# The state products of the first scan of a hybrid layer, as three one-pass products of split operands

## Chip, cores and metric

The kernel runs on one core of a Trainium2 chip. The metric is the device time of one execution in microseconds (us). Of each kernel several executions are timed, and their median is given. A separate execution is recorded by the hardware profiler, and all durations of single instructions come from it.

## What is computed

The reference is one layer of a hybrid decoder: 1024 tokens with 16 learned tokens ahead, model width 1024, all in float32. A state-space group (16 heads of 64, state size 128, in two groups of 8 heads) and an attention group stand side by side, their outputs are mixed by one matrix, and a gated feed-forward layer with a short convolution follows. What matters here is the state-space part, which works in chunks of 128 tokens (the 16 learned tokens are a short chunk of their own, chunk 0):

```python
states = jnp.einsum('bclgn,bgjcl,bclgjp->bcgjpn', Bc, decay_states, Xdt)
chunk_decay = jnp.exp(Acs[..., -1])
def step(carry, inp):
    st, dec = inp
    return carry * dec[..., None, None] + st, carry
_, prev = lax.scan(step, init, (states..., chunk_decay...))
y_off = jnp.einsum('bclgn,bcgjpn,bgjcl->bclgjp', Cc, prev, jnp.exp(Acs))
y = (y_diag + y_off).reshape(Bsz, Lp, H, P)[:, pad:]
```

For each group and chunk there are so two products with the state: `states`, from B and the decayed, time-scaled X of the chunk, and `y_off`, from C and the state before the chunk.

## The kernel before, in words

Everything is kept with channels or tokens on the 128 partitions. A large product such as x times a weight block is done on TensorE in the type fp32r, which takes one pass: each operand is split into a rounded part ("hi", a copy on ScalarE) and the rest ("lo", a subtraction, mostly on GpSimd), and hi·hi, lo·hi and hi·lo are summed in PSUM. `project_steps` (L165) is that loop for the projections, in three column blocks of 400, 384 and 256 tokens; `load_w` (L151, L152) splits the weights.

The scan of group g runs over chunks c = 0 to 8 in `scan_steps`, with three parts:

- `chunk_weights(g, c)`: builds the decay matrix of the chunk. Eight copies `sgh` on ScalarE (L615) and one product `sgl` on GpSimd (L617) are the two parts of a moving operand, TensorE sums them into `sg` (L624), ScalarE takes the exponential `em` (L626). TensorE also makes `cb` (L628), VectorE masks it to `cbm` and multiplies it into `em` (L630, L631). `xdt` (L634, VectorE) and `yo` (L637, GpSimd) scale the chunk's X.
- `chunk_outputs(g, c)`: `yf` = C times the state `prev` (L652), scaled to `yt` and added into `yo` (L654, L656); `xw` = decayed X (L660); `st` = B times `xw` (L663); the new state `pv` = old state times the chunk's decay (L668, GpSimd) plus `st` (L671, VectorE).
- `chunk_store(g, c)`: the product `yt` of `em` and `xdt` with the transposed `yo` added in PSUM (L682, L685), gated to `zk` (L689), squared to `sqk` (L692) and summed over heads (L694, L697), and stored.

The products `yf` and `st` have operands in plain fp32. The trace records each as two matmuls of 128x512.

The order of calls is: weights of chunk c+1, then one or two steps of other work, outputs of c, then one or two steps, store of c. The other work (`fill`) in the first group's scan is the projection, convolution (L465, L468 on VectorE, activation L470) and transposition (`tt_X`, L476, L481) of the second group's X blocks, then its z blocks; in the second group's scan it is the projection of q, k and v. So projections keep TensorE busy between the pieces of a scan. In this part of the program no order is written out by hand: the framework plans the order on each engine from its own estimates, with earlier calls first among those that it takes for ready. Later, the attention has TensorE's order by hand, and the feed-forward part that of four engines.

Buffers: the pool `sp` gives a tag one slot unless `bufs` says otherwise. `sgh` and `sgl` (128 x 1024 each) have one slot, `em`, `xdt`, `yo`, `xk`, `zk` and `prev` two. PSUM has two slots of tag `sd` for `yf` and `st`. The tags `bt`, `bn` and `ct` (B, B by tokens, and C) have one slot, and the second group's are written into it.

Of the kernel before, what the change touches and what calls it, by code (L numbers as in the profile page):

```python
# [9 lines left out]
F32 = mybir.dt.float32  # L10
F32R = mybir.dt.float32r
BF16 = mybir.dt.bfloat16
AF = mybir.ActivationFunctionType
ALU = mybir.AluOpType
# [3 lines left out]
P = 128  # L18
# [35 lines left out]
def tile_layer(ctx: ExitStack, tc: tile.TileContext, x, meta, rows, parts,  # L54
               w_z, w_xbc, w_dt, w_q, w_k, w_v, w_out, w_up, w_down, out):
    nc = tc.nc
    mm = nc.tensor.matmul
# [16 lines left out]
    def psum_sd(name):  # L74
        return stage[0][1].tile([P, 512], F32, tag="sd", name=name, bufs=2)
# [377 lines left out]
    with tc.tile_pool(name="ssd", bufs=1, side="right") as sp:  # L453
# [149 lines left out]
        def chunk_weights(g, c):  # L603
# [34 lines left out]
                                    op=ALU.mult)  # L638
            return em, xdt, yo

        def chunk_outputs(g, c, em, xdt, yo, prev):
            bt, bn, ct = state[g]
            nr = NM if c == 0 else P
            c0 = 0 if c == 0 else NM + (c - 1) * P
            hs = slice(8 * g, 8 * g + 8)
            nm = f"{g}_{c}"
            y0 = M0 if c == 0 else 0
            zk = sp.tile([P, 4, P], F32, tag="zk", name=f"zk{nm}", bufs=2)
            nc.sync.dma_start(out=zk[:, :, y0:nr], in_=zd[g][:, :, c0 + y0:c0 + nr].rearrange("b p t -> p b t"))
            if c > 0:  # L650
                yf = psum_sd(f"yf{nm}")
                mm(yf[:nr], ct[:, c0:c0 + nr], prev, start=True, stop=True)  # L652
                yt = sp.tile([P, 8, 64], F32, tag="yt", name=f"yt{nm}")
                nc.vector.tensor_tensor(yt[:nr], yf[:nr].rearrange("p (h d) -> p h d", d=64),  # L654
                                        eac[:nr, c, hs].unsqueeze(2).to_broadcast([nr, 8, 64]), op=ALU.mult)
                nc.vector.tensor_tensor(yo[:nr], yo[:nr], yt[:nr], op=ALU.add)  # L656
            nprev = None
            if c < NT:
                xw = sp.tile([P, 8, 64], F32, tag="xw", name=f"xw{nm}")
                nc.vector.tensor_tensor(xw[:nr], xdt[:nr],  # L660
                                        dec[:nr, c, hs].unsqueeze(2).to_broadcast([nr, 8, 64]), op=ALU.mult)
                st = psum_sd(f"st{nm}")
                mm(st, bn[:nr, c, :], xw[:nr].rearrange("p h d -> p (h d)"), start=True, stop=True)  # L663
                nprev = sp.tile([P, 512], F32, tag="prev", name=f"pv{nm}", bufs=2)
                if c == 0:
                    nc.vector.tensor_copy(nprev, st)
                else:
                    nc.gpsimd.tensor_tensor(nprev.rearrange("p (h d) -> p h d", d=64),  # L668
                                            prev.rearrange("p (h d) -> p h d", d=64),
                                            cdec[:, c, hs].unsqueeze(2).to_broadcast([P, 8, 64]), op=ALU.mult)  # L670
                    nc.vector.tensor_tensor(nprev, st, nprev, op=ALU.add)  # L671
            return yo, zk, nprev
# [29 lines left out]
        def scan_steps(g):  # L702
            cur = chunk_weights(g, 0)
            prev = None
            yield
            for c in range(NT + 1):
                nxt = chunk_weights(g, c + 1) if c < NT else None
                yield
                yo, zk, prev = chunk_outputs(g, c, *cur, prev)
                yield  # L710
                chunk_store(g, c, cur[0], cur[1], yo, zk)
                cur = nxt
# [364 lines left out]
    def psum_fa(name):  # L1077
        return stage[0][1].tile([P, 2, 512], F32, tag="fa", name=name, bufs=3)
# [8 lines left out]
    op = opool.enter_context(tc.tile_pool(name="outp", bufs=2, side="right"))  # L1087
# [13 lines left out]
    acc = psum_fa("halo1")[:, 0, 0:256]  # L1101
# [688 lines left out]
    for s in range(n2):  # L1790
        n, a, b, p = steps2[s]
# [29 lines left out]
        for _ in range(2 if s > 5 and s % 2 else 1):  # L1821
            if wload and (wload[0][0] is not None or s > 5):
                pool, nm, k = wload.pop(0)
# [87 lines left out]
```

## Time and profile before

| What | us |
|---|---|
| median of three executions | 1728.21 |
| lowest, highest | 1726.89, 1728.25 |
| profiled execution | 1726.21 |
| its span, from the first to the last instruction | 1724.3 |
| granted TensorE clock, mean | 0.998 |

The profile counts an engine as busy when an instruction of it runs; register, semaphore and DMA-issuing instructions don't count. PE is TensorE's matmul side, PEld its weight loads, DVE is VectorE, ACT is ScalarE, POOL is GpSimd. A line such as "L652" is the line of the kernel. In a view of waits, "A <- B" says that A's engine stood idle until B ended. In a timeline a row is one instruction or a few alike: its start, its duration, its engine. Matmuls are pipelined, so that two rows may overlap; the distance from one start to the next tells what a matmul costs in a stream.

### The profile page before, as it was taken

To read this page: it belongs to the slowest core of one execution; us is meant where nothing else is said; L and a number is where in the kernel's file an instruction comes from. 1 tells how busy PE (TensorE), PEld (TensorE's weight loads), DVE (VectorE), ACT (ScalarE), POOL (GpSimd) and SP (SyncE) were. 2 spreads that over 40 slices of the span, in tenths; PEclk is the share of its full clock that TensorE was granted. 3 is DMA by queue.
4 is the path that set the end of the run, shared out by engine and by line. 5 is a ranking of instruction groups with operands and counts; after the bars stand their busy time and mean duration, and the time that the engine had idled before them with its cause. 6 is when DMAs were issued, how large, how long until landed. Compare 5 with 4: busy or idle time off the path is not lost. (4 is left out here: it accounts for less than half of the span.)

```text
span 1724.3 us, 28047 instructions
## 1 busy us (share of the span) xinstructions
PE 1703.0 (99%) x11230; PEld 1496.2 (87%) x11230; DVE 1117.8 (65%) x1233; ACT 821.2 (48%) x1370; POOL 850.4 (49%) x642
## 2 busy tenths in 40 slices
PE   7999999999999999999999999999999999999998
PEld 6999889888999998998788788999888888887886
DVE  5752973875676677578530567676666666658777
ACT  5423663555566566557652344433333333344544
POOL 4323664585566575565552122587767777400001
PEclk9999999999999999999999999999999999999999
DMA  4233343231011101112214653233332223395334
GB/s 164 58 111 98 105 127 108 68 105 38 26 38 38 36 28 38 38 50 86 64 68 147 212 174 123 73 107 110 103 92 92 92 92 99 118 330 180 105 113 179
DMA packets 90674, 173.87 MB, mean 101 GB/s; under 512 B 10704, under 2 KB 35816, under 8 KB 90544
## 3 DMA queue, kind: packets, MB, share of 16 engines
q1 hardware_dynamic: 90544, 172.08, 31.4%
q8 instruction: 88, 1.44, 0.4%
q14 instruction: 42, 0.34, 0.1%
HBM read 122.32 MB, written 49.73 MB: 100 GB/s over the span
## 5 line engine op out<-in xcount | busy, mean ns | idle before, releaser
L782 POOL TENSOR_TENSOR bt<-bt,kp 128x256 f32<-128x256 f32 (+7 forms) x128 | 213.0, 1683 | 185.7 <-DVE kp L780 144.3
L780 DVE TENSOR_TENSOR_SCAN kp<-kp,hold 128x272 f32<-128x272 f32 (+7 forms) x128 | 183.5, 1474 | 24.7 <-ACT kp L773 14.3
L1265 POOL TENSOR_TENSOR wlo<-wr,whi 128x1024 fp32r<-128x1024 f32 x43 | 107.7, 2516 | 37.8 <-ACT whi L1264 37.8
L1768 POOL TENSOR_TENSOR fms<-fms 128x1 f32<-128x1 f32 x8 | 2.6, 331 | 223.8 <-ACT dh L1653 197.1
L773 ACT ACTIVATE kp<-z 128x288 f32<-128x288 f32 (+6 forms) x112 | 82.6, 737 | 50.5 <-PE z L772 27.8
L1264 ACT ACTIVATE whi<-wr 128x1024 fp32r<-128x1024 f32 x43 | 45.6, 1060 | 111.5 <-PE fX L1322 67.9
L165 PE MATMUL pj_k<-xs,wh_k 128*128 128x400 f32 (+2 forms) x384 | 95.6, 336 | 0.0
L165 PE MATMUL pj_v<-xs,wh_v 128*128 128x400 f32 (+2 forms) x384 | 95.0, 334 | 0.0
L1394 DVE SCALAR_TENSOR_TENSOR ga<-gr,pp,ga 128x1024 f32<-128x1024 f32 x44 | 71.8, 1632 | 35.1 <-ACT ga L1387 34.3
L165 PE MATMUL pj_q<-xs,wh_q 128*128 128x386 f32 (+2 forms) x384 | 93.8, 331 | 0.0
L796 ACT ACTIVATE th<-tw 128x1024 f32<-128x1024 f32 (+2 forms) x96 | 75.6, 815 | 37.4 <-PE tw L794 37.3
L1653 ACT ACTIVATE dh<-ar 128x512 fp32r<-128x512 f32 x77 | 48.6, 631 | 92.9 <-PE dnB L1731 44.7
L165 PE MATMUL pj_X<-xs,wh_X 128*128 128x400 f32 (+2 forms) x384 | 92.0, 326 | 0.0
L165 PE MATMUL pj_z<-xs,wh_z 128*128 128x386 f32 (+2 forms) x384 | 91.6, 326 | 0.0
L748 DVE CAST qh<-q 128x128 fp32r<-128x128 f32 x64 | 45.5, 712 | 69.9 <-PE z L772 69.6
L1654 DVE TENSOR_TENSOR dl<-ar,dh 128x512 fp32r<-128x512 f32 x77 | 53.2, 691 | 50.2 <-ACT dh L1653 50.2
L966 PE MATMUL mo<-woa,yh 128*128 128x512 f32 x256 | 85.2, 400 | 0.0
L774 ACT ACTIVATE bt<-z 128x288 f32<-128x288 f32 (+6 forms) x112 | 82.9, 740 | 0.0
L794 PE MATMUL tw<-ident,bt 128*128 128x128 f32 x576 | 75.9, 274 | 2.2 <-POOL bt L782 1.6
L809 PE MATMUL av<-th,v 128*64 128x128 f32 x1152 | 77.2, 278 | 0.0
L809 PEld LDWEIGHTS av<-th,v 128*64 128x64 f32 x1152 | 61.5, 136 | 13.8 <-issue 10.9
L794 PEld LDWEIGHTS tw<-ident,bt 128*128 128x128 f32 x576 | 65.5, 141 | 8.6 <-issue 4.0
(560 smaller groups left out, 5623.9 us busy)
## 6 DMA issues: line engine op xcount, KB each, us to landing
wr<-in_w_up SPq DMA_DIRECT2D x44, 512.0 KB
fds<-ga SPq DMA_DIRECT2D x44, 256.0 KB
b<-in_w_down SPq DMA_DIRECT2D x44, 256.0 KB
ar<-fds SPq DMA_DIRECT2D x44, 256.0 KB
fda<-ga SPq DMA_DIRECT2D x33, 256.0 KB
ar<-fda SPq DMA_DIRECT2D x33, 256.0 KB
yk<-yd SPq DMA_DIRECT2D x16, 512.0 KB
wor<-in_w_out SPq DMA_DIRECT2D x12, 512.0 KB
```

What stands on the lines that cost most here:

```text
L165: mm(acc[:ncol, :n - s], a[:, k, :ncol], xs[c0][:, b, k, s:n], start=(k == 0 and j == 0), stop=(k == KB - 1 and j == 2))
L773: nc.scalar.activation(kp[:, :, a:a + w], z[:, :, :w], AF.Sigmoid, scale=-QSCALE)
L774: nc.scalar.activation(bt[:, :, a:a + w], z[:, :, :w], AF.Sigmoid, scale=QSCALE)
L780: nc.vector.tensor_tensor_scan(kp[:, j][:, ::-1], kp[:, j][:, ::-1], hold[:, L - n:L][:, ::-1], 0.0, op0=ALU.mult, op1=ALU.max)
L782: nc.gpsimd.tensor_tensor(bt[:, j, 0:m], bt[:, j, 0:m], kp[:, j, 1:m + 1], op=ALU.mult)
L794: nc.tensor.transpose(tw[:, j, b, :], bt[:, j, c0:c0 + P], ident)
L796: nc.scalar.activation(th[:, :, :nb, :], tw[:, :, :nb, :], AF.Copy)
L809: mm(av[halves[j], :], v[:, kb, halves[j]], th[:, j, b, :], start=kb == 0, stop=kb == i)
L966: recent[0] = mm(acc, u[:, k, :], v[:, cs], start=(k == 0 and j == 0), stop=(k == 7 and j == 2))
L1265: nc.gpsimd.tensor_tensor(l, raw, h.bitcast(F32), op=ALU.subtract)
L1394: nc.vector.scalar_tensor_tensor(v, self.g[jj][:, :, i:i + 256], fconv_w[:, j, i:i + 1], v, op0=ALU.mult, op1=ALU.add)
L1654: sub(lo[:, k], raw, hi[:, k].bitcast(F32), op=ALU.subtract)
```

## The change

For group 0 alone, `yf` (chunks 1 to 8) and `st` (chunks 1 to 7) are made of three fp32r products each. A new helper splits each operand: a copy on ScalarE into a rounded part and a subtraction on GpSimd for the rest, both anew in each chunk. The parts of ct and bn get tags of their own (one slot each, 128 x 2 x 128). The parts of the wide operands, 128 x 2 x 512, go into the slots of `sgl` (for prev) and `sgh` (for xw). Chunk 0's `st` and all of group 1 stay as they were.

```diff
+        def parts_of(src, tag, name, shape):
+            t = sp.tile([P, 2] + shape, F32R, tag=tag, name=name)
+            nr = src.shape[0]
+            nc.scalar.activation(t[:nr, 0], src, AF.Copy)
+            nc.gpsimd.tensor_tensor(t[:nr, 1], src, t[:nr, 0].bitcast(F32), op=ALU.subtract)
+            return t[:nr, 0], t[:nr, 1]
+
+        def product3(acc, u, v):
+            for i, (a, b) in enumerate(((0, 0), (1, 0), (0, 1))):
+                mm(acc, u[a], v[b], start=i == 0, stop=i == 2)
...
             if c > 0:
                 yf = psum_sd(f"yf{nm}")
-                mm(yf[:nr], ct[:, c0:c0 + nr], prev, start=True, stop=True)
+                if g == 0:
+                    product3(yf[:nr], parts_of(ct[:, c0:c0 + nr], "ctp", f"ctp{nm}", [P]),
+                             parts_of(prev, "sgl", f"pvp{nm}", [512]))
+                else:
+                    mm(yf[:nr], ct[:, c0:c0 + nr], prev, start=True, stop=True)
...
                 st = psum_sd(f"st{nm}")
-                mm(st, bn[:nr, c, :], xw[:nr].rearrange("p h d -> p (h d)"), start=True, stop=True)
+                xw2 = xw[:nr].rearrange("p h d -> p (h d)")
+                if g == 0 and c > 0:
+                    product3(st, parts_of(bn[:, c, :], "bnp", f"bnp{nm}", [P]), parts_of(xw2, "sgh", f"xwp{nm}", [512]))
+                else:
+                    mm(st, bn[:nr, c, :], xw2, start=True, stop=True)
```

## The prediction

> **What bounds the kernel now.** I read the page first, then the waits of TensorE's weight loads over the whole span, then the busy time by stage, and last the timelines of the scan's engines.
>
> ```profile
> span 1724.3 us, 28047 instructions
> ...
> PE 1703.0 (99%) x11230; PEld 1496.2 (87%) x11230; DVE 1117.8 (65%) x1233; ACT 821.2 (48%) x1370; POOL 850.4 (49%) x642
> ```
>
> TensorE is busy for 1703.0 of 1724.3 us. Since a matmul's end is modelled, that share alone doesn't show that TensorE is the limit; its waits do. In the next view each row gives the waiting instruction, what released it, the sum in us, the number of waits and the longest.
>
> ```profile
> PEld xtp L285 <- DVE xn L273: 10.7, 5, 8.4
> ...
> PEld tt_X L481 <- DVE xtk L477: 1.0, 6, 0.2
> ...
> PEld sg L624 <- ACT sgh L615: 0.6, 2, 0.4
> ```
>
> The only large wait is at the program's start. Around the scan, TensorE waits for other engines in pieces of 0.2 to 0.4 us. So in that stage TensorE's own work sets the time: what leaves its queue is gained, and what makes its queue stand is lost. The first group's scan runs from 150 to about 290 us. Busy time by stretch there, and in the second group's scan (the columns are: length; then PE, PEld, DVE, ACT, POOL; clock; DMA share; GB/s):
>
> ```profile
> 165.00:240.00 75.00, 75.00 (x494) 65.91 (x493) 66.38 (x68) 45.55 (x86) 49.03 (x37) 1.00 0.35 99
> 240.00:285.00 45.00, 45.00 (x299) 40.96 (x297) 20.04 (x23) 18.53 (x39) 21.51 (x19) 1.00 0.39 125
> ...
> 320.00:400.00 80.00, 80.00 (x537) 66.70 (x535) 57.73 (x71) 40.02 (x101) 63.83 (x59) 1.00 0.33 93
> ```
>
> TensorE is full in all three. Between 165 and 240 us VectorE is nearly full too (66.4 of 75 us), because there it also convolves the second group's X blocks; GpSimd has 26 us left. That stretch is where the change can hurt.
>
> **The change part by part: TensorE.** Fifteen products change: yf of chunks 1 to 8 and st of chunks 1 to 7. The timeline shows what one costs now (start, duration, engine, line, operation), and what a one-pass matmul of the same size costs where many follow each other:
>
> ```profile
> 178.65 1.02 PE L652 MATMUL yf<-pv,ct 128*128 128x512 f32 x2
> 179.50 1.02 PE L663 MATMUL st<-xw,bn 128*128 128x512 f32 x2
> ```
>
> ```profile
> 1600.05 0.39 PE L1731 MATMUL dnB<-dh 128*128 128x512 f32 x1
> ...
> 1602.31 0.39 PE L1731 MATMUL dnB<-dh,dl 128*128 128x512 f32 x1
> ```
>
> The product st begins 0.85 us after yf. Ten one-pass steps lie between 1600.05 and 1602.31, so one is 0.226 us and three are 0.68 us. Each product gains 0.17 us and fifteen gain **2.6 us**. The trace of before has no three-pass product in the scan, so a bound from the other side is wanted. The slowest one-pass step of 512 columns near it is this one:
>
> ```profile
> 186.37 0.48 PE L624 MATMUL sg<-sgh,lowr 128*128 128x512 f32 x1
> 186.68 0.39 PE L624 MATMUL sg<-sgl,lowr 128*128 128x512 f32 x1
> ```
>
> At 0.31 us a pass, a product would take 0.93 us, and fifteen would lose 1.2 us. I take 0.226, because the three passes stand among projections that are one-pass as well, while the 0.31 follows the transposes of yt.
>
> **ACT and POOL.** Each product splits two operands: a copy to the rounded part on ScalarE and a subtraction on GpSimd, one pair 128x128 (ct or bn), one 128x512 (prev or xw). The nearest groups of the scan, as busy us and mean ns:
>
> ```profile
> L615 ACT ACTIVATE sgh<-tri,adh 128x128 fp32r<-128x128 f32 x64 | 20.0, 391 | 0.0
> ...
> L692 ACT ACTIVATE sqk<-zk 128x512 f32<-128x512 f32 x8 | 5.0, 629 | 13.0 <-DVE zk L689 13.0
> ```
>
> ```profile
> L637 POOL TENSOR_TENSOR yo<-xk,dskip 128x512 f32<-128x512 f32 x8 | 10.1, 1263 | 6.1 <-PE yt L685 6.1
> ...
> L697 POOL TENSOR_TENSOR sq<-sqk 128x128 f32<-128x128 f32 x7 | 5.8, 828 | 0.5
> ```
>
> ScalarE gets 0.39 + 0.63 = 1.02 us a product, 15.3 us in all. GpSimd gets 0.83 + 1.26 = 2.09 us a product, 31.4 us in all. Ten of the products (chunks 1 to 5) fall between 165 and 240 us: GpSimd goes from 49.0 to 69.9 of 75 us, ScalarE from 45.6 to 55.8. The other five bring GpSimd from 21.5 to 32.0 of 45. Everything fits, so this work costs nothing by itself; its cover is that the projections keep TensorE busy meanwhile. No DMA is added or moved.
>
> **The new waits.** The wide parts of prev live in the slot of sgl, and those of xw in that of sgh, each a single buffer. Three orders become forced within a chunk c: the parts are written after the segment matmuls sg of chunk c+1; yf and st wait for the parts; and sgh, sgl of chunk c+2 wait until st and yf have read them. Behind a late sgh on ScalarE stand the evictions of the projections, and behind a late sgl on GpSimd the low weight parts; TensorE waits for both.
>
> The second hand-over, st to the next sg, shows in the weight loads:
>
> ```profile
> 196.56 0.19 PEld L663 LDWEIGHTS st<-xw,bn 128*128 128x128 f32 x1 [0.24 <-issue]
> ...
> 200.19 0.09 PEld L476 LDWEIGHTS tt_X<-ident,xsT 128*16 128x16 f32 x1
> ...
> 201.31 0.19 PEld L624 LDWEIGHTS sg<-sgh,lowr 128*128 128x128 f32 x1
> ```
>
> The weight load at 196.56 is that of st's second half, so st ends about 0.85 us later, and 3.9 us are left up to sg. Eight sgh copies need at most 8 x 0.39 = 3.1 us, and sgl runs beside them. It fits with 0.8 us to spare, where before they were prepared ahead of st.
>
> The first hand-over, sg to yf, is tightest at chunk 5:
>
> ```profile
> 233.73 0.38 PE L628 MATMUL cb<-ct,bt 128*128 128x128 f32 x2
> ...
> 237.37 1.02 PE L652 MATMUL yf<-pv,ct 128*128 128x512 f32 x2
> ```
>
> That is 3.6 us after the last sg. The parts of ct and bn have slots of their own and can be ready. Needed are prev's copy and rest, 0.63 + 1.26 = 1.9 us, behind two exponentials of em, of the size of the sqk row, 0.63 us each: 3.2 us. The rest of xw follows 1.26 us later, 4.4 us against 4.3 at which st would now start. So I charge 0.2 us for each of the three tight chunks (3, 5 and 7, the ones with one projection step in this gap), **0.6 us**; the ends are nothing and, at every product, the 0.46 us by which a GpSimd operation varies (below).
>
> Sum: -2.6 + 0.6 = -2.0 us. The profiled execution took 1726.21 us, its span 1724.3 and 1.9 around it; it would become 1724.2. The median of the three runs, 1728.21, lies 2.0 above that execution, so the forecast for a median is **1726.2 us**, a gain of 0.12%.
>
> **The rivals.** The first ends on the other side: *VectorE falls behind because GpSimd holds it up.* The same operations with and without company:
>
> ```profile
> 187.35 1.53 DVE L634 TENSOR_TENSOR xdt<-xk,dt 128x512 f32<-128x512 f32 x1
> ...
> 245.02 0.69 DVE L634 TENSOR_TENSOR xdt<-xk,dt 128x512 f32<-128x512 f32 x1 [3.50 <-PE yt L682]
> ```
>
> ```profile
> 186.83 1.50 POOL L637 TENSOR_TENSOR yo<-xk,dskip 128x512 f32<-128x512 f32 x1
> ...
> 245.64 1.04 POOL L637 TENSOR_TENSOR yo<-xk,dskip 128x512 f32<-128x512 f32 x1 [0.88 <-PE yt L685]
> ```
>
> Beside each other xdt loses 0.84 us and yo 0.46 us; apart, neither does. If each added GpSimd operation held VectorE for its full length, 20.9 us would be added between 165 and 240 us, where VectorE has 75 - 66.4 = 8.6 us spare. It would be 12.3 us late. What TensorE reads of VectorE's chain is tt_X, and the X block's activation ends before it here:
>
> ```profile
> 196.01 1.07 ACT L470 ACTIVATE xsT<-xsT 128x1040 f32<-128x1040 f32 x1 [1.27 <-DVE xsT L468]
> ```
>
> It ends at 197.1, 3.1 us ahead of the transposes at 200.2. So TensorE would stand 12.3 - 3.1 = 9.2 us, and the sum is -2.6 + 9.2 = +6.6 us: **1734.8 us**. It decides from the point at which VectorE loses more than (8.6 + 3.1) / 20.9 = 0.56 of each added GpSimd microsecond. The rows above show 0.84 / 1.50 = 0.56: just at the edge. Against it: some added operations fall where VectorE itself waits. I give it 0.22. The Trainium skill, "SBUF — State Buffer", section "SBUF: two separate sides", states that VectorE operations with two SBUF inputs and GpSimd operations share a port pair as an exclusive lock, so that the later one blocks fully. By that rule the full 20.9 us would count and the time would be the 1734.8; the row's 0.84 of 1.50 us agrees with blocking, but not with a full loss for each operation.
>
> The second: *the hand-overs are late at every chunk.* In the scan no order is written by hand; the framework plans each engine's order beforehand. If it puts the products where it expects the parts, and GpSimd takes 1.50 instead of 1.04 us, two rests in a row are 0.92 us late in each of 7.5 chunks: 6.9 us, and -2.6 + 6.9 = +4.3: **1732.5 us**. For it speaks that sgh and sgl lose their lead; against it, that the projection steps ahead of yf leave 4 to 8 us in most chunks. 0.15.
>
> The third: *the product doesn't become cheaper*, at 0.31 us a pass: +1.2, **1729.4 us**, 0.07. The fourth: *the new plan also removes waits*, the 1.0 and 0.6 us of the tt_X and sg rows: -2.6 - 1.6 = -4.2, **1724.0 us**, 0.10; nothing in the profile asks for it.
>
> **How the numbers follow.** The forecast holds 0.46. About 0.2% (3.5 us) is what a measurement of this kernel can tell from no change. The forecast's own range is 1724.5 to 1728.5; it gives 0.38 within 0.2%, 0.05 faster and 0.03 slower. The port rival gives 0.20 slower and 0.02 within, the late hand-overs 0.13 and 0.02, the dear product 0.07 within, the better plan 0.10 faster. In sum: faster 0.15, within 0.49, slower 0.36. The range goes from 1722 (the better plan, less the spread of runs) to 1737 (both waits in part).
>
> **What would show it.** Right: in the new trace successive passes of yf stand 0.23 us apart, the waits of yf, st and sg for POOL and ACT are below 1 us together, and GpSimd shows about 70 of 75 us between 165 and 240 us. The port rival would show as waits of tt_X or yt for DVE or ACT of several us, with VectorE full. Late hand-overs would show as waits of yf or st for POOL and of sg for sgh or sgl, at most chunks. I am wrong altogether if the later stages, whose inputs and order this change hardly touches, move by more than the scan.

## The result

The changed kernel takes 1745.87 us (median of four executions, 1744.08 to 1748.91), the kernel before in the same comparison 1727.69 us. The ratio is 1.0111 with a 95% interval of 1.0099 to 1.0124: 18 us slower, where 2 us faster was forecast. The profiled execution took 1748.91 us, so its trace holds about 3 us more than the median.

The page of the changed kernel, and its busy time in the three stretches that the prediction showed of the kernel before:

```profile
span 1747.2 us, 28132 instructions
...
PE 1713.0 (98%) x11245; PEld 1505.1 (86%) x11245; DVE 1123.3 (64%) x1233; ACT 833.2 (48%) x1400; POOL 877.8 (50%) x672
```

```profile
165.00:240.00 75.00, 67.25 (x431) 60.45 (x430) 58.93 (x55) 40.99 (x79) 57.10 (x45) 0.95 0.29 79
240.00:285.00 45.00, 42.40 (x275) 37.99 (x274) 24.41 (x31) 30.77 (x63) 34.06 (x33) 0.96 0.39 123
...
320.00:400.00 80.00, 77.09 (x483) 64.53 (x483) 59.63 (x77) 41.81 (x106) 55.49 (x45) 0.96 0.28 76
```

TensorE was full in all three; now it stands for 7.75, 2.6 and 2.9 us. And the granted clock, 1.00 before, is 0.95 and 0.96: in some places it is at half rate for 3.4 or 6.8 us. At half rate TensorE takes nearly twice as long. The two matmuls of chunk 0's `st` in the second group's scan, the same in both kernels, took 1.12 us before and 2.07 us here. Half rate costs nothing while TensorE stands. Counted in steps of half a microsecond, as the busy time times what the clock lacks of 1.00, it costs at most 2.2 and 1.7 us in the first group's scan and 3.4 us in the second's.

Two marks that both kernels have place the loss. The first projection of q starts at 309.8 us before and at 324.4 after: 14.6 us are lost up to the end of the first scan. Of these 10.4 of standing and 3.9 of clock, less 2.4 for the gain of the passes, make 11.9; the other 2.7 us show in neither. The attention's first product starts at 400.0 and 420.6: 6.0 us more are lost in the second group's scan, whose code is unchanged (2.9 of standing and 3.4 of clock make 6.3). The last 2.3 us of the 22.9 come later.

What TensorE's matmuls waited for in the changed kernel, over the whole program (the sum in us, the number of waits, the longest):

```profile
PE yf L650 <- POOL pvp L645: 5.4, 3, 4.3
PE sg L624 <- ACT sgh L615: 2.9, 3, 1.9
PE st L650 <- POOL xwp L645: 2.0, 2, 1.7
PE tt_X L481 <- DVE xtk L477: 1.5, 3, 0.5
```

Of the 2.9 us of sg, 2.4 are in the second group's scan; in the first, sg waits for sgh once, for 0.6 us.

The longest wait, at chunk 3, shows how such a wait arises. First TensorE's row, then GpSimd's rows, then ScalarE's and VectorE's rows beside them, then the stretches with the clock:

```profile
217.65 0.79 PE L650 MATMUL yf<-pvp,ctp 128*128 128x512 f32 x1 [4.35 <-POOL pvp L645]
```

```profile
208.19 1.50 POOL L637 TENSOR_TENSOR yo<-xk,dskip 128x512 f32<-128x512 f32 x1
211.59 2.39 POOL L713 TENSOR_TENSOR sqk<-sqk 128x128 f32<-128x128 f32 x2 [1.89 <-ACT sqk L711]
214.06 1.32 POOL L716 TENSOR_TENSOR sq<-sqk 128x128 f32<-128x128 f32 x1
215.34 2.26 POOL L645 TENSOR_TENSOR pvp<-pv,pvp 128x512 fp32r<-128x512 f32 x1
217.56 1.27 POOL L645 TENSOR_TENSOR xwp<-xw,xwp 128x512 fp32r<-128x512 f32 x1
218.79 1.89 POOL L617 TENSOR_TENSOR sgl<-tri,adl 128x1024 fp32r<-128x1024 f32 x1
```

```profile
210.88 0.63 ACT L711 ACTIVATE sqk<-zk 128x512 f32<-128x512 f32 x1 [3.26 <-DVE zk L708]
```

```profile
213.59 1.47 DVE L631 TENSOR_TENSOR em<-em,cbm 128x1024 f32<-128x1024 f32 x1
214.99 1.49 DVE L468 SCALAR_TENSOR_TENSOR xsT<-craw_X,pp,xsT 128x1040 f32<-128x1040 f32 x1
```

```profile
205.00:215.00 10.00, 8.30 (x56) 6.97 (x55) 9.81 (x10) 4.45 (x8) 8.03 (x7) 1.00 0.55 160
215.00:220.00 5.00, 2.35 (x6) 1.86 (x7) 2.40 (x4) 1.50 (x2) 5.00 (x4) 0.52 0.20 52
220.00:225.00 5.00, 5.00 (x26) 4.75 (x24) 2.10 (x3) 3.21 (x9) 3.00 (x4) 0.79 0.00 0
```

The rest of prev (pvp) stands in GpSimd's queue behind the sums of squares of an earlier chunk, which nobody needs soon. These in turn waited 1.89 us for ScalarE, which had waited 3.26 us for VectorE's zk. And pvp itself takes 2.26 us, where the rest of xw (xwp), of the same size, takes 1.27; for the first half of it VectorE runs the operation at 214.99. The third pass of yf needs that rest, and every projection behind it on TensorE stands for 4.35 us. The clock is at half rate from 215.2 us, while TensorE still stands, to 222.0, so that TensorE works for 4.4 us at half rate. The slot of sgl comes free only after yf, so sgl is built last of all, at 218.79; here it was still in time, for the next sg, at 226.4, had no wait. Another slot is held as well: in the first scan VectorE stands 6.6 us in three waits before it may write the next xw, until GpSimd has taken the rest from the last one.

The Trainium skill, "TensorE: Matmul & The Clock Gate", Part 1, names a full and a half rate and has the clock at half after at least one idle window of about 3.4 us. The 4.35 us are longer than that, but here the clock fell 1.9 us after TensorE had begun to stand, and in the run e10 below a wait of 2.16 us has half rate behind it. So less than a whole window was enough here, and the measurement decides.

### The profile page after: what moved, and what is told of

It reads as the page before. It is cut to its first block, busy times and chain, and to the rows that moved or that the text cites. A ratio compares the mean times of both kernels' runs of the same rounds, so it can differ in the third digit from the quotient of the medians.

```text
span 1747.2 us, 28132 instructions
## 1 busy us (share of the span) xinstructions
PE 1713.0 (98%) x11245; PEld 1505.1 (86%) x11245; DVE 1123.3 (64%) x1233; ACT 833.2 (48%) x1400; POOL 877.8 (50%) x672
```

## The experiments

Each line of the table is one kernel, with its median, and its ratio to the kernel before as run on the same chip. The last column is taken from the one profiled execution: the time from the start of the first projection of z to that of the first projection of q, which holds the whole first scan and leaves out what happens later. It is 203.1 us in the kernel before. e1, e7 and e8 leave out parts of the computation: e1 the real operands, e7 and e8 the rests.

| Kernel | us | ratio (95% interval) | first z to first q, us |
|---|---|---|---|
| the change | 1745.87 | 1.0111 (1.0099 to 1.0124) | 217.4 |
| e1: passes only | 1726.04 | 0.9994 (0.9984 to 1.0003) | 201.5 |
| e2: splits only | 1739.82 | 1.0079 (1.0061 to 1.0097) | 214.7 |
| e3: own slots | 1734.79 | 1.0043 (1.0029 to 1.0056) | 211.5 |
| e4: rests on VectorE | 1734.43 | 1.0041 (1.0028 to 1.0055) | 209.7 |
| e5: own slots, early | 1734.50 | 1.0047 (1.0033 to 1.0062) | 210.0 |
| e6: own slots, rests on VectorE | 1732.38 | 1.0030 (1.0020 to 1.0040) | 208.9 |
| e7: own slots, no rests | 1726.72 | 0.9991 (0.9980 to 1.0002) | 201.6 |
| e8: shared slots, no rests | 1726.04 | 0.9995 (0.9985 to 1.0004) | 202.1 |
| e9: own slots, chunks 5 to 8 | 1730.50 | 1.0018 (1.0008 to 1.0028) | 203.8 |
| e10: before, with the subtractions | 1731.53 | 1.0030 (1.0019 to 1.0041) | 208.2 |
| e12: own slots, rests on VectorE, chunks 5 to 8 | 1730.38 | 1.0018 (1.0009 to 1.0028) | 203.6 |
| e13: own slots, chunks 6 to 8 | 1726.84 | 0.9999 (0.9990 to 1.0007) | 202.2 |

Four theories stood against each other: the rests come late through GpSimd's queue (late hand-over), the shared slots hold back sgh and sgl, added GpSimd work holds VectorE up (the port), and the three passes are no cheaper.

**e1, the passes alone.** The products take slices of an input that is long there.

```diff
-                    product3(yf[:nr], parts_of(ct...), parts_of(prev, ...))
+                    f = xs[0].rearrange("p a b c -> p (a b c)")
+                    product3(yf[:nr], (f[:, 0:P], f[:, P:2 * P]), (f[:, 512:1024], f[:, 1024:1536]))
...
-                    product3(st, parts_of(bn...), parts_of(xw2, ...))
+                    product3(st, (f[:, 0:P], f[:, P:2 * P]), (f[:, 512:1024], f[:, 1024:1536]))
```

> The fifteen products are three one-pass matmuls each, but their operands are slices of the normalized input, which is long there: nothing is split, and yf and st are not the real products. If three passes are as cheap as 3 x 0.226 us and everything else is the waits and the split work, this gains about 2.6 us on the kernel before (about 1725). If the passes are dear in this place (0.31 us each), it loses about 1 us. If the change hurts because three passes disturb TensorE's queue or clock by themselves, a good part of the 18 us shows here.

The timeline of TensorE in e1:

```profile
195.45 0.86 PE L650 MATMUL yf<-xs 128*128 128x512 f32 x3
196.15 0.85 PE L650 MATMUL st<-xs 128*128 128x512 f32 x3
196.84 0.39 PE L165 MATMUL pj_X<-xs,wh_X 128*128 128x256 f32 x2
```

A product takes 0.70 us where it took 0.85: 0.16 less, fifteen times, 2.4 us. The median gains 1.0 us, with an interval from a gain of 0.16% to a loss of 0.03%; the stage of the last column is 1.6 us shorter. So the passes are as cheap as forecast, the gain of the whole kernel is at the edge of what can be measured, and the passes themselves do no harm.

**e2, the splits alone.**

```diff
-                    product3(yf[:nr], parts_of(ct...), parts_of(prev, ...))
+                    parts_of(ct[:, c0:c0 + nr], "ctp", f"ctp{nm}", [P])
+                    parts_of(prev, "sgl", f"pvp{nm}", [512])
+                    mm(yf[:nr], ct[:, c0:c0 + nr], prev, start=True, stop=True)
```

(and alike for st)

> All splits of the change are made, in the same shared slots, but yf and st stay the old fp32 products of the unsplit operands. Theory of the late hand-over (TensorE's queue stands because the rests, queued on GpSimd behind the sums of squares, are not ready, and the clock then falls): most of the loss goes, at most 5 us above before, with sg waiting a little since sgh and sgl still come after the parts in their slots. Theory of the shared port (added GpSimd work holds VectorE up): nearly all of the 18 us stays, with waits of TensorE for VectorE's tiles. Theory of the shared slots: also most of it stays, as waits of sg for sgh and sgl.

Two thirds of the loss stay although no product reads the parts (in the stage of the last column 11.6 of 14.3 us). So TensorE's direct wait for the rests isn't needed for it. Its waits in e2, in the scan:

```profile
PE pj_X L165 <- ACT craw_X L211: 2.7, 1, 2.7
PE sg L624 <- ACT sgh L615: 2.4, 1, 2.4
PE tt_X L481 <- DVE xtk L477: 2.1, 2, 1.8
```

The projection waits for ScalarE's eviction, sg for its operand, and the X block's transposition for VectorE. That fits both the slots and the port. This run also began the z projections 2.8 us later than the kernel before, ahead of the scan; 2.8 of its 12.8 us are of that kind.

**e3, own slots.**

```diff
-            t = sp.tile([P, 2] + shape, F32R, tag=tag, name=name)
...
+        def prev_parts(prev, nm):
+            return split2(prev, part("pvh", f"pvh{nm}", 512), part("yt", f"pvl{nm}", 512))
+        def xw_parts(xw2, nm):
+            return split2(xw2, part("xwh", f"xwh{nm}", 512), part("xk", f"xwl{nm}", 512, 2))
```

> As the change, but the wide parts have slots of their own (the rest of xw in that of xk, that of prev in that of yt), so sgh and sgl can be built ahead again as in the kernel before; the four small tiles of the dt stage moved into other slots to make room. Theory of the shared slots: the loss goes, 1725 to 1730. Theory of the late hand-over: sg no longer waits, but yf and st still wait for the rests on GpSimd, since these stand behind the same operations: 1735 to 1745. Theory of the port: no change, 1746.

11 of the 18 us are gone, and with them all waits for parts and for sgh. (The parts of e3 have slots apart from sgh and sgl; the rests share those of yt and xk.) What is left, in the same stretch of 75 us, is mostly waiting for VectorE:

```profile
PE yt L709 <- DVE yo L676: 3.9, 1, 3.9
PE tt_X L481 <- DVE xtk L477: 1.7, 2, 1.5
```

All three forecasts missed: the shared slots alone would have taken the whole loss away, the late hand-over had named yf and st, which no longer wait, and the port had named no change of the time. The port's sign of e2, waits for VectorE's tiles, came. The longest group of VectorE between 165 and 240 us, first in the kernel before, then in e3, then in e7 (below, without the subtractions) and in e10 (below, the kernel before with them):

```profile
L468 DVE SCALAR_TENSOR_TENSOR xsT<-craw_X,pp,xsT 128x1040 f32<-128x1040 f32 x12 | 20.5, 1707 | 0.2
```

```profile
L468 DVE SCALAR_TENSOR_TENSOR xsT<-craw_X,pp,xsT 128x1040 f32<-128x1040 f32 x12 | 24.4, 2034 | 0.2
```

```profile
L468 DVE SCALAR_TENSOR_TENSOR xsT<-craw_X,pp,xsT 128x1040 f32<-128x1040 f32 x12 | 20.3, 1696 | 0.2
```

```profile
L468 DVE SCALAR_TENSOR_TENSOR xsT<-craw_X,pp,xsT 128x1040 f32<-128x1040 f32 x12 | 24.5, 2040 | 0.2
```

The same twelve operations take 0.33 us more each, 3.9 us in all, with the subtractions and not without them. Not every group grows: the four operations of L465 take 5.9 us in e3 and 7.9 before. The clock is at half rate again during and after the wait of 3.9 us, as the next row of e3 shows; after the wait of 1.5 us it had stayed at 1.00.

```profile
220.00:225.00 5.00, 3.82 (x14) 3.44 (x15) 4.55 (x6) 3.98 (x8) 5.00 (x5) 0.50 0.00 2
```

**e4, the rests on VectorE** (shared slots).

```diff
-            nc.gpsimd.tensor_tensor(t[:nr, 1], src, t[:nr, 0].bitcast(F32), op=ALU.subtract)
+            nc.vector.tensor_tensor(t[:nr, 1], src, t[:nr, 0].bitcast(F32), op=ALU.subtract)
```

> As the change, but the rests are subtracted on VectorE instead of GpSimd. Theory of the late hand-over through GpSimd's queue: the waits for the rests become shorter, 1730 to 1738, unless VectorE, full between 165 and 240 us, is the later one. Theory of the port: GpSimd is back at its old load, but VectorE gets some 10 us more in that stretch, beyond its 8.6 us of spare time: about as slow as the change, with waits for VectorE's tiles.

1734.4 us, as the late hand-over had forecast: away from GpSimd's queue, the shared slots lose little. TensorE now waits for VectorE's rests, 3.0 us before st and 2.4 before yf.

**e5, own slots and the splits a chunk earlier.** The parts for chunk c + 1 are made at the end of `chunk_outputs(0, c)`.

```diff
+            if g == 0 and c < NT:
+                early_parts(c + 1, nprev, nxt[1])
             return yo, zk, nprev
```

> Own slots as in the run before, and besides each chunk's operands are split at the end of the chunk before, so that nothing can be late by the order alone. Theory of the late hand-over: the rest of the loss goes, about 1725. Theory of the port: the same amount of GpSimd work still falls into the stretch where VectorE is full, so the time stays near that of the own slots, 1732 to 1737, with waits of TensorE for VectorE's tiles.

1734.5 us, the time of the own slots alone, as the port had forecast. Its trace has no wait for a part, but again one of yt for VectorE's yo, 3.9 us as in e3. So it isn't the order of the code that costs the rest of the loss; that the load itself does fits.

**e6, own slots and the rests on VectorE.** The edit is that of e4 in e3.

> Own slots, and the rests on VectorE. The parts of the loss that come from sharing the slots and from GpSimd's extra work are both taken away; VectorE gets about 0.69 + 0.28 us a product. Theory of the port: a rest costs VectorE less as its own work (0.97 us a product) than as GpSimd's neighbour (up to 2 us), so faster than with own slots alone: 1727 to 1732. If VectorE's own load is what counts, as slow or slower than own slots alone, 1734 or more.

1732.4 us, 2.4 below e3 and 0.4 above the upper end of the port's forecast. The intervals of the two overlap, so that the medians don't show that the rests cost less as VectorE's own work; the stage of the last column is 2.6 us shorter, in one execution each.

**e7, own slots and no rests.** The cut is against e3; the rounded part stands in for the rest, and the rests' slots go with them.

```diff
-        def split2(src, hi, lo):
+        def part(src, tag, name, n):
+            hi = sp.tile([P, n], F32R, tag=tag, name=name)
             nc.scalar.activation(hi, src, AF.Copy)
-            nc.gpsimd.tensor_tensor(lo, src, hi.bitcast(F32), op=ALU.subtract)
-            return hi, lo
...
+            return hi, hi
```

> Own slots, three passes, copies on ScalarE, but no rests at all: the rounded part stands in for the rest, which leaves the rests out of the computation. It tells what GpSimd's 15 x 2 subtractions cost. Theory of the port: without them VectorE is as before, and the gain of the passes is seen, 1725 to 1727. If the copies or the order of the passes are what is left of the loss, it stays at 1732 to 1735.

1726.7 us: without the thirty subtractions the loss is gone, by 8.1 us against e3. The copies on ScalarE cost nothing that can be seen.

**e10, the kernel before with the subtractions.**

```diff
+        def idle_sub(src, n, nm):
+            t = sp.tile([P, n], F32R, tag=f"idle{n}", name=f"idle{n}_{nm}")
+            nc.gpsimd.tensor_tensor(t, src, src, op=ALU.subtract)
...
+                if g == 0:
+                    idle_sub(ct[:, c0:c0 + nr], P, nm)
+                    idle_sub(prev, 512, nm)
                 mm(yf[:nr], ct[:, c0:c0 + nr], prev, start=True, stop=True)
```

(and alike for st)

> The kernel before, with the 30 subtractions of the change added on GpSimd at the same places (of each operand from itself, into a tile that nobody reads); no copies, no three passes, no shared slots, and no one waits for them. Theory of the port: VectorE is held up between 165 and 240 us all the same, 1732 to 1738, with waits of TensorE for VectorE's tiles there. Theories of the late hand-over or of the slots: within 2 us of before.

Work on GpSimd whose results nobody reads costs 0.30% (0.19% to 0.41%), about 5 us, a little less than the port's 1732 to 1738. It is less work in the scan than the expectation says: the fifteen small subtractions, of ct and bn, run between 65 and 105 us, ahead of the scan, so that only the fifteen of 128x512 fall beside it. Its stretch of 75 us, and TensorE's waits in it:

```profile
165.00:240.00 75.00, 71.79 (x462) 63.35 (x462) 66.60 (x62) 40.12 (x75) 59.95 (x44) 0.98 0.31 89
```

```profile
PE tt_X L481 <- DVE xtk L477: 3.2, 2, 2.2
```

TensorE stands 3.2 us and loses at most 1.7 us by the clock, at just the place that the port rival had named: the transposed X block on VectorE. The longer of the two waits, with VectorE's and GpSimd's rows ahead of it and the clock behind it:

```profile
221.57 2.97 DVE L631 TENSOR_TENSOR em<-em,cbm 128x1024 f32<-128x1024 f32 x1 [1.07 <-ACT em L626]
```

```profile
221.56 1.89 POOL L617 TENSOR_TENSOR sgl<-tri,adl 128x1024 fp32r<-128x1024 f32 x1
```

```profile
224.79 0.66 PE L481 MATMUL tt_X<-ident,xsT 128*128 128x128 f32 x4 [2.16 <-DVE xtk L477]
```

```profile
225.00:230.00 5.00, 5.00 (x22) 5.00 (x21) 4.96 (x5) 1.36 (x2) 3.62 (x3) 0.66 0.69 169
```

The em of the chunk before took 1.48 us. Here sgl began with it, em took 2.97, and the copy that TensorE waits for came behind em. VectorE waits for no result of GpSimd in this scan, so that a late GpSimd isn't what holds it up.

**e8, shared slots and no rests.**

```diff
-            nc.gpsimd.tensor_tensor(t[:nr, 1], src, t[:nr, 0].bitcast(F32), op=ALU.subtract)
-            return t[:nr, 0], t[:nr, 1]
+            return t[:nr, 0], t[:nr, 0]
```

> The change with its shared slots, but without the rests (the rounded part stands in for them; they are left out of the computation). With the own slots this step went from 1734.8 to 1726.7. If the shared slots cost their 11 us by themselves, since sgh and sgl are built too late, 1735 to 1738 with waits of sg for sgh. If they cost that only because the rests, queued behind other work on GpSimd, hold the slots long, 1725 to 1728.

1726.0 us. Shared slots by themselves cost nothing that can be seen. Six kernels now stand in a square, by their medians:

| rests | none | on VectorE | on GpSimd |
|---|---|---|---|
| own slots | 1726.7 | 1732.4 | 1734.8 |
| shared slots | 1726.0 | 1734.4 | 1745.9 |

Sharing costs -0.7, 2.0 and 11.1 us, of which the first two are within the noise. By the stage of the first scan alone it costs 0.5, 0.8 and 5.9 us: of the 11.1 about half is lost in the first scan, and 6.0 in the second group's, as told below. So the loss in the first scan belongs to neither the slots nor the rests alone. It fits that a slot is held until the rest has come through GpSimd's queue and been read, as the rows of the longest wait show.

**e9, e12, e13, the late chunks.** e9 is e3, and e12 is e6, with `c > 4` added to both conditions; e13 is e3 with `c > 5`.

> Own slots, rests on GpSimd, but three passes only for chunks 5 to 8, whose products come when VectorE has finished with the X blocks (busy for 20 of 45 us there). Theory of the port: nothing is held up that TensorE reads, and seven products gain 0.16 us each: 1 us faster than before, 1725 to 1727. If the rests cost wherever they stand, 1728 to 1731.

> As the run with the late chunks alone, the rests on VectorE. Theory of the port: VectorE has 25 us to spare there and gets 7; about 1 us faster than before, 1725 to 1727, and no worse than with the rests on GpSimd.

> As the run with the late chunks, but only chunks 6 to 8 are changed, so that no split falls beside the X blocks at all. In the run with chunks 5 to 8, TensorE waited 1.7 us for the last X block in the scan, and 2.9 us for GpSimd much later, in the attention, whose order on the engines is planned anew with each edit. If the port beside the X blocks was the first of these, the wait for X is gone here and the first projection of q begins 0.8 us or more ahead of the 309.8 us of the kernel before; five products gain 0.8 us, 1726 to 1727, unless the attention stands again: then up to 1730.

e9 and e12 are 0.18% slower, against the port's forecast of a gain; e9 is in the range that would mean that the rests cost wherever they stand. In the trace of e9 TensorE waits 1.7 us for the last X block, at which chunk 5 still falls; the first projection of q comes 1.1 us late. But the attention's last product comes 4.8 us late (896.8 against 892.0), so most is lost in the attention. One wait there is longer:

```profile
PE tw L818 <- POOL cb L807: 2.9, 1, 2.9
```

The kernel before waits 1.6 us at tw, and its clock falls behind it too. What e9 has more up to the last product is two stretches of 3.4 us at half rate with no standing ahead, at 417 and 881 us, of at most 1.7 us each. Such stretches are not e9's own (see the last section), and this execution, of 1732.43 us, is one of the slowest of e9's twelve, so the trace doesn't explain its median.

In e13 the wait for X is gone, as the port theory says, and q begins 0.7 us earlier (309.1), where 0.8 was forecast; its time is that of the kernel before within 0.1%. No version beat the kernel before by more than can be measured. Why e9 and e12 are slower than e13 later on stays open.

## Why the prediction was wrong

**What bounds the kernel: right.** TensorE's standing and its clock account for most of the loss, and the scan lost more (14.6 us) than the later stages (8.3 us).

**The passes: right.** 0.17 us a product was forecast, 0.16 measured, 2.4 us instead of 2.6.

**"Everything fits, so this work costs nothing by itself": wrong.** It compared GpSimd's 69.9 us with the 75 of the stretch. But GpSimd and VectorE slow each other, and VectorE was nearly full already. Half of the rests alone cost 5 us without anyone reading them (e10), and all of them 8.1 us with own slots (e3 against e7). The port rival had this mechanism and its place, and put it at 9.2 us of standing; in e10 TensorE stood 3.2 us. It was given 0.22 because its rows stood "just at the edge", at 0.84 / 1.50 = 0.56. But of the 1.50 us GpSimd itself had lost 0.46 beside VectorE; against the 1.04 that it takes apart, 0.84 is 0.81. That, and VectorE at 66.4 of 75 us, should have weighed more.

**The first hand-over, 0.6 us: wrong by its size.** It measured 7.4 us (5.4 before yf and 2.0 before st), most of it at chunk 3, one of the three that the step had called tight; chunk 1, not among them, has 1.7. The step counted the parts' own durations, and the two exponentials ahead on ScalarE, but not what stands ahead of the rests on GpSimd. The rows above show it: sums of squares of an earlier chunk, themselves waiting for ScalarE and so for VectorE. Nor did it count that the rest itself takes 2.26 us beside VectorE in place of 1.26.

**The second hand-over, nothing: nearly right.** In the first scan sg waited for sgh once, for 0.6 us. The longer waits of sg came in the second group's scan, where no slot is shared.

**The rivals as alternatives: wrong.** The port and the late hand-overs were priced one by one and given separate chances. They came together and raised each other: in the first scan the rests cost 9.9 us with own slots (211.5 against 201.6), and sharing the slots with them 5.9 more. So the upper end of 1737 was too low.

**What no step had: the clock, and the next stage.** A wait of 3.9 or 4.35 us came with a clock of 0.50 to 0.52; in the first scan the clock took up to 3.9 us beside 10.4 of standing. And the second group's scan, unchanged, lost 6.0 us. There a VectorE operation on the way to its first chunk came 0.1 us after a GpSimd operation instead of together with it. First the kernel before, VectorE and GpSimd, then the changed kernel:

```profile
310.60 1.01 DVE L468 SCALAR_TENSOR_TENSOR ct<-craw_C,pp,ct 128x784 f32<-128x784 f32 x1
```

```profile
310.59 3.29 POOL L152 TENSOR_TENSOR wl_v<-wr_v,wh_v 128x1024 fp32r<-128x1024 f32 x1 [9.02 <-ACT wh_v L151]
```

```profile
325.28 3.12 DVE L468 SCALAR_TENSOR_TENSOR ct<-craw_C,pp,ct 128x784 f32<-128x784 f32 x1
```

```profile
325.18 2.39 POOL L152 TENSOR_TENSOR wl_v<-wr_v,wh_v 128x1024 fp32r<-128x1024 f32 x1 [9.02 <-ACT wh_v L151]
```

Before, VectorE took 1.01 us and GpSimd 3.29; after, VectorE 3.12 and GpSimd 2.39. One of the two ran at its own pace, and the other took longer by about that time. The activation of C's last part then starts about 3 us later, counted from the first projection of q (at 8.8 instead of 5.8 us behind it), and sg of the second scan waits for sgh. All twelve traces of the experiments have 1.01 and 3.29 or 3.30 here, and in them the time from the first projection of q to the attention's first product is 90.0 to 90.2 us, as before; the changed kernel alone has 3.12, and 96.2. So this part of the loss looks like bad luck in a start and not like a price of the change. That the one delay caused all of the 6.0 us is argued from the traces; it was not tried by itself, nor is it known whether the three executions without a profile had it.

## What to carry to other kernels

A gain in passes on a full engine is worth what its preparation leaves of it. Work put on another engine's queue has to be asked three things: what stands ahead of it there, whom it slows beside it, and which slot is held until it is read. Where the bounding engine stands for 2 us or more, reckon with the clock falling behind it: in the two scans of this case the clock added up to 7.3 us to 13.3 of standing. No sharp limit can be read off: the clock fell behind one wait of 2.2 us (e10) and behind three close together of 1.45 us in all (at 252.7 us in the changed kernel), and not behind one of 1.7 (e9). To weigh changes of a few microseconds, time the stage beside the whole: two marks in a trace showed the gain of e1 (1.6 us), which the medians left open, though from one execution each. Price rivals that can occur together also as a sum.

## What was not expected of the hardware

That VectorE and GpSimd hold each other up can be seen in single rows: 1.01 us became 3.12, by a difference of a tenth of a microsecond in the start. The Trainium skill, "SBUF — State Buffer", section "SBUF: two separate sides", has an exclusive lock, which whoever starts first holds for the whole instruction. The two rows of the changed kernel agree with it: GpSimd is 0.10 us ahead, and the 2.1 us that VectorE loses are close to the 2.39 that GpSimd ran. In the two rows of the kernel before GpSimd loses 0.9 us, about VectorE's 1.01, but their recorded starts are 0.01 us apart, GpSimd's ahead, too close to tell who was first.

The clock also fell with no standing ahead that the trace shows. Around the start of the attention, TensorE is busy throughout, in the changed kernel and in e8 alike (the stretch first of the changed kernel, then of e8):

```profile
410.00:440.00 30.00, 30.00 (x216) 26.80 (x215) 14.16 (x30) 13.35 (x24) 17.95 (x27) 0.95 0.19 54
```

```profile
410.00:440.00 30.00, 29.95 (x230) 26.85 (x229) 19.72 (x22) 17.93 (x32) 19.17 (x15) 0.94 0.07 19
```

The profiled execution of the kernel before has 1.00 there. Each such fall is 3.4 us long and costs at most 1.7 us. Six of the fourteen traces have one there, 16 to 18 us after the attention's first product, and ten have one 475 to 480 us after that product, again with no standing ahead. Other executions of the kernel before may have them too: in the run of e12 it took from 1723.70 us at a mean clock of 0.999 to 1730.35 at 0.996. So such falls may belong to an execution and not to a change; their cause is open.
